# Encoder trunk on one core: the engine that evacuates a transpose is picked by slot instead of by a running count

## The chip, the cores and the metric

The kernel runs on one core of a Trainium2 chip. The metric is device time of one execution, in microseconds (us). The engines are PE (matmuls and transposes), DVE (VectorE), ACT (ScalarE), POOL (GpSimd) and SP, which only issues DMAs here.

## What is computed

Two layers of an encoder over 2048 tokens of width 1024, float32. Each layer normalises x, projects it, runs four groups of attention heads (A dense, B sliding window, C neighbourhood with a bias, D differential), gates each, and projects back:

```python
h = _rmsnorm(x, norm_g[l]); z = h @ w_in[l]
o_a = dense softmax(q_a k_a^T) v_a            # 4 query heads on 2 key-value heads
o_b = softmax over a window of +-128 keys, with a sink logit
o_c = softmax over an 8 x 16 neighbourhood, with rpb_c
o_d = (softmax(q1 k1^T) - lam * softmax(q2 k2^T)) v_d
mix = concat(o_a*silu(g_a), o_b*silu(g_b), o_c*silu(g_c), o_d*silu(g_d))
x = x + mix @ w_out[l]
```

## The kernel before

Tokens go in 16 tiles t of 128. A layer has four stages: the D projections (with the output projection of the layer before), D attention with the other projections threaded in, the phase of the A, B and C heads, and the output projection. The change is in the third, which takes about 530 us of each layer.

That phase makes two **sweeps** over the 16 query tiles. Sweep 1 pairs A's key-value head 0 with the B heads, sweep 2 pairs A's key-value head 1 with the C heads. One query tile of a sweep is a **group** of three units: an A unit (two query heads against 2048 keys) and two small units (two heads each, three blocks of 128 keys for B, three or four of 120 for C). A unit has scores (S, Sb or Sc, matmuls into PSUM), a maximum and a copy to SBUF on DVE (L497, L1007, L1043), one `exp` on ACT per head (L504 for A, 2048 wide; L1018 and L1051 for the small units), transposes of the probabilities on PE, an evacuation of the transposes from PSUM to SBUF, and the product with v (L520, L539).

`drive` writes PE's order by hand, and in this phase PE keeps that order. It runs one group's transposes while it computes the next group's scores. A **slot** is one call of `front`: up to four transposes into one PSUM tile PTp (L513 or L531), an evacuation, then one score unit of the next group. The A unit has slots 0 to 7 of a group, the first small unit slots 8 and 9, the second slots 10 and 11 (in groups 0 and 15 of sweep 1 the small units have one slot each: 8 and 9). After the last slot come the products L520 and L539, and then the next group's slot 0. `k_build` puts four transposes of keys (kT, L98) ahead of slot 3 or slot 6 in sweep 1: one build in groups 1, 3, 4, 6 and 9, two in groups 5 and 11 to 14. A build of B or C keys takes four steps on ACT and DVE in turn (L959, L960, L962, L963), one of A keys two (L962, L963).

PTp tiles come from `tpool`, which hands out two turns of a PSUM pool of two buffers (it also holds kT) and then one of a pool of one. Scores have three PSUM buffers. Only PE's order is fixed: DVE, ACT, POOL and SP take the order that a scheduler gives them when the program is built, so the change moves instructions there.

Evacuations go through `evac`. Its third argument was a period: `ev[0]` counts all evacuations of a layer, D's 256 included, and every third goes to DVE (L472), the rest to ACT (L474):

```python
ev[0] += 1
if mode and ev[0] % mode == 0:
    V.tensor_copy(dst, src)
else:
    A.copy(dst, src)
```

As a group has twelve slots, the count falls on the same slots again and again: 0, 3, 6 and 9 in groups 1 to 15 of sweep 1, and 2, 5, 8 and 11 in sweep 2 (1, 4 and 7 in group 0 of sweep 1). All D evacuations have mode 0 and are ACT's.

Of the kernel before, what the change touches and what calls it, by code (L numbers as in the profile page):

```python
# [27 lines left out]
GAP2 = 2  # L28
GAP3 = 0
KQ = 5  # L30
EVB = 3
EVC = 3
MS0 = 2
WPT = 13
WOU = 360
KA0 = 16
FR2 = 12.2
EV3 = 3
EVA1 = 3
SC64 = 64.0 ** -0.5  # L40
SC32 = 32.0 ** -0.5
NEG = -1e30
# [35 lines left out]
def trunk_kernel(ctx, tc, x, norm_g, w_in, w_out, qn_a, kn_a, sink_b, rpb_c, lam_q1, lam_k1, lam_q2, lam_k2,  # L78
# [180 lines left out]
    for l in range(depth):  # L259
# [91 lines left out]
        dv = dvx.enter_context(tc.tile_pool(name="dv", bufs=2, reuse_waits="tile"))  # L351
        with tc.tile_pool(name="wd", bufs=16, reuse_waits="tile") as wp, tc.tile_pool(name="st", bufs=3, reuse_waits="tile") as st:
# [84 lines left out]
            for t in range(NT):  # L437
                h = hs.pop(t)
                if t == WPT:
                    wb = big.tile([128, 4, 2, 256], F32R, tag="b", name="wb")  # L440
                    for k in range(4):
                        s = st.tile([128, 384], F32, tag="st", name="wst")
# [17 lines left out]
        with tc.tile_pool(name="sm", bufs=6, reuse_waits="tile") as sm, \  # L460
# [1 line left out]
                tc.tile_pool(name="sps", bufs=3, space=PSUM, reuse_waits="tile") as sps, tc.tile_pool(name="ops", bufs=1, space=PSUM, reuse_waits="tile") as ops, \  # L462
                tc.tile_pool(name="tps2", bufs=2, space=PSUM, reuse_waits="tile") as tps:
            later = []
            ev = [0]
            vt, kt = {}, {}
            tpool = cycle([tps])

            def evac(dst, src, mode):
                ev[0] += 1  # L470
                if mode and ev[0] % mode == 0:
                    V.tensor_copy(dst, src)  # L472
                else:
                    A.copy(dst, src)  # L474
# [32 lines left out]
            def dense_front(u, i):  # L507
                p, c = u["p"], slice(i * 256, (i + 1) * 256)
                tp = next(tpool).tile([128, 512], F32, tag="t", name="PTp")
                for h in range(2):  # L510
                    for a in range(2):
                        j = i * 2 + a
                        PE.transpose(tp[:, (h * 2 + a) * 128:(h * 2 + a + 1) * 128], p[:, h, j * 128:(j + 1) * 128], idn)  # L513
                evac(p[:, :, c], tp.rearrange("p (h k) -> p h k", h=2), u["ev"])

            def dense_back(u):
                js = range(NT) if u["fixed"] else range(NT - 1, -1, -1)
# [5 lines left out]
            def small_front(u, i):  # L523
                ws, n, kw = u["ws"], u["n"], u.get("kw", 128)
                js = [j for j in (2 * i, 2 * i + 1) if j < n]
                if i == 0:
                    u["pt"] = u["ptp"].tile([128, 1024], F32, tag="pt", name="PT")
                tp = next(tpool).tile([128, 512], F32, tag="t", name="PTp")
                for a, j in enumerate(js):
                    for h in range(2):  # L530
                        PE.transpose(tp[0:kw, (a * 2 + h) * 128:(a * 2 + h + 1) * 128], ws[h][:, j * kw:(j + 1) * kw], idn)  # L531
                w = len(js) * 256
                evac(u["pt"][0:kw, i * 512:i * 512 + w], tp[0:kw, 0:w], u["ev"])

            def small_back(u):
                n, kw = u["n"], u.get("kw", 128)
# [188 lines left out]
            with tc.tile_pool(name="st2", bufs=5, reuse_waits="tile") as st, tc.tile_pool(name="w2", bufs=10, reuse_waits="tile") as wp, \  # L725
# [177 lines left out]
                with tc.tile_pool(name="bb", bufs=1, reuse_waits="tile") as bbp, tc.tile_pool(name="p1", bufs=1, reuse_waits="tile") as p1p:  # L903
                    kds = {(0, 0): kd0[0], (0, 1): kd0[1]}

                    def get_kd(kv):
                        def f(c):
                            if (kv, c) not in kds:
                                k_ = big2.tile([128, S], F32R, tag="b", name="kdt")
                                nc.sync.dma_start(out=k_.bitcast(F32), in_=kd_d[0][:, c, :])  # L910
                                kds[kv, c] = k_
                            return kds[kv, c]
                        return f
                    units = [dict(kv=kv, t=t, k=get_kd(kv), qp=dv, s=d_scores, par=True, ns=16, nv=8, ev=0, fin=fin_d, fb=6 + kv,
                                  p1=p1p, fixed=False, front=dense_front, back=dense_back, get_o=own_o,
                                  v=lambda h, j, kv=kv: vd[:, j, kv * 64:(kv + 1) * 64]) for kv in range(2) for t in range(NT)]

                    for u in units:
                        u["fp"] = lambda: tps.tile([128, 512], F32, tag="t", name="fin")
                    for u in units[-2:]:  # L920
                        u["fp"] = lambda: zps.tile([128, 256], F32, tag="z", name="fin")
                    drive([[u] for u in units], GAP2, fill, FR2)
# [133 lines left out]
                yield  # L1056

            def a_unit(kv, t, q, pre):
                return dict(kv=kv, t=t, s=a_scores, par=True, ev=EVA1 if kv else EV3, ns=8, nv=8, fin=fin_plain, fb=kv, q=q, pre=pre,
                            front=dense_front, back=dense_back, get_o=own_o, oc=0, fixed=True, fd=4,  # L1060
                            v=lambda h, j: vt["A"][:, j, kv * 64:(kv + 1) * 64])

# [5 lines left out]
            o_bc = []  # L1068

            def small_unit(sc, i, t, q, px, fb, ns, nv, bias=None, pre=lambda: None):  # L1070
                return dict(kv=i, t=t, s=sc, par=False, ev=EVC if sc is c_scores else EVB, ns=ns, nv=nv, fin=fin_plain, fb=fb, q=q, pp=px, bias=bias, pre=pre,
                            front=small_front, back=small_back, get_o=pair_o, oc=128 * i, ptp=ptp, fd=5 + 2 * i)

            with tc.tile_pool(name="qst", bufs=2, reuse_waits="tile") as qst, tc.tile_pool(name="ql", bufs=2, reuse_waits="tile") as ql, \
# [63 lines left out]
                units = []  # L1138
                for ps in range(2):
                    for t in range(NT):  # L1140
                        units.append(a_unit(ps, t, lambda t=t, ps=ps: qq["A", ps, t], lambda t=t, ps=ps: prep(ps, t + 1)))
                        for i in range(2):
                            if ps == 0:
                                units.append(small_unit(b_scores, i, t, lambda t=t: qq["B", 0, t], px, 2 + i, 2,
                                                        (min(t + 2, NT) - max(t - 1, 0) + 1) // 2))
                            else:
                                units.append(small_unit(c_scores, i, t, lambda t=t: qq["C", 1, t], px, 4 + i, 2, 2,
                                                        lambda t=t, i=i: get_bias(t, i)))
                                units[-1]["cm"] = cm
# [49 lines left out]
```

## Time and profile before

| | |
|---|---|
| Time, median of 3 runs (lowest, highest) | 3598.17 us (3595.62, 3601.56) |
| The profiled execution's own time | 3600.7 us |
| Its span in the trace | 3598.7 us |
| Busy: PE, DVE, ACT, POOL | 3449.8, 2503.0, 2097.6, 955.6 us |
| Granted clock of PE, mean | 0.986 |

The span is from the first to the last instruction; the 2.0 us between it and the time lie around the trace. A busy PE is one that has a matmul in its pipeline, and the ends of matmuls are modelled, so lost time shows better in the distance between two starts than in the idle time.

### The profile page before, as it was taken

The numbers are of one execution on the slowest core, as the hardware profiler recorded it, in microseconds if no ns is written. First come the engines' busy times: TensorE is split into PE (matmuls) and PEld (weight loads), VectorE is DVE, ScalarE is ACT, GpSimd is POOL, SyncE is SP. The second block draws the span as 40 slices with busy tenths as digits, with TensorE's granted clock in tenths as the row PEclk, the third lists the DMA queues.
The fourth block names the chain that finished last, engine by engine and source line by source line (L and its number), as shares of the span: only waits on it lengthen the run. The fifth ranks groups of instructions, "written<-read, shape, count | busy, mean of one in ns | idle before, by whom it ended". The sixth has DMA issues, their size and how long they took to land. (4 is left out here: it accounts for less than half of the span.)

```text
span 3598.7 us, 71627 instructions
## 1 busy us (share of the span) xinstructions
PE 3449.8 (96%) x25232; PEld 2969.7 (83%) x25232; DVE 2503.0 (70%) x7829; ACT 2097.6 (58%) x3961; POOL 955.6 (27%) x1604
## 2 busy tenths in 40 slices
PE   8989999999989999999999899999999799899999
PEld 8979898888967777877899798988889577678787
DVE  4387878777877887774234878787777787777733
ACT  4455666556667776771144556665666677777711
POOL 4465324643100001001044553255331100000000
PEclk9999999999999999999999999999999999999999
DMA  4542325332233244335445323253231332543343
GB/s 146 186 113 85 85 80 175 86 91 77 62 95 84 81 122 121 88 100 178 147 132 180 96 79 92 70 181 88 79 87 57 97 86 82 135 111 96 90 158 113
DMA packets 355777, 387.47 MB, mean 108 GB/s; under 512 B 59802, under 2 KB 298586, under 8 KB 350298
## 3 DMA queue, kind: packets, MB, share of 16 engines
q1 hardware_dynamic: 351098, 367.17, 35.1%
q10 hardware_dynamic: 4320, 15.73, 1.3%
q8 instruction: 199, 3.26, 0.4%
q14 instruction: 160, 1.31, 0.1%
HBM read 258.83 MB, written 123.91 MB: 106 GB/s over the span
## 5 line engine op out<-in xcount | busy, mean ns | idle before, releaser
L497 DVE TENSOR_SCALAR_CACHE_REDUCE P<-S 128x512 f32<-128x512 f32 x1536 | 1018.5, 686 | 238.8 <-PE S L496 172.4
L319 PE MATMUL z<-wt,ht 128*128 128x256 f32 (+1 forms) x3008 | 892.5, 298 | 8.6 <-ACT wt L310 4.1
L321 PE MATMUL z<-wt,ht 128*128 128x256 f32 (+1 forms) x3008 | 885.5, 295 | 4.0 <-DVE wt L313 4.0
L323 PE MATMUL z<-wt,ht 128*128 128x256 f32 (+1 forms) x3008 | 884.1, 294 | 0.0
L513 PE MATMUL PTp<-idr,P 128*128 128x128 f32 x4096 | 632.3, 278 | 38.9 <-ACT P L474 19.8
L474 ACT COPY P<-PTp 128x512 f32<-128x512 f32 x864 | 491.3, 584 | 291.9 <-PE PTp L513 289.0
L504 ACT ACTIVATE P<-P,nm 128x2048 f32<-128x2048 f32 x256 | 513.8, 2007 | 180.5 <-DVE jk L503 172.1
L513 PEld LDWEIGHTS PTp<-idr,P 128*128 128x128 f32 x4096 | 495.4, 143 | 137.0 <-ACT P L474 28.0
L319 PEld LDWEIGHTS z<-wt,ht 128*128 128x128 f32 x3008 | 570.1, 190 | 28.4 <-ACT wt L310 4.5
L321 PEld LDWEIGHTS z<-wt,ht 128*128 128x128 f32 x3008 | 571.0, 190 | 18.4 <-DVE wt L313 6.2
L323 PEld LDWEIGHTS z<-wt,ht 128*128 128x128 f32 x3008 | 570.9, 190 | 7.0
L496 PE MATMUL S<-kA,q 128*128 128x512 f32 x1024 | 364.1, 438 | 8.3 <-DVE P L497 8.3
L222 PE MATMUL y<-wot,ms 128*128 128x512 f32 x1440 | 331.1, 392 | 0.6 <-DVE ms L212 0.6
L222 PEld LDWEIGHTS y<-wot,ms 128*128 128x128 f32 x1440 | 270.7, 188 | 60.7 <-DVE ms L212 1.0
L544 POOL TENSOR_TENSOR gg<-gt,rzh 128x128 f32<-128x128 f32 x192 | 77.3, 403 | 911.7 <-DVE rzh L606 385.9
L312 POOL TENSOR_SCALAR wt<-wst,g 128x256 fp32r<-128x256 f32 (+1 forms) x336 | 215.2, 652 | 363.8 <-PE z L323 263.0
L721 DVE SCALAR_TENSOR_TENSOR P<-P,cf,P 128x2048 f32<-128x2048 f32 x128 | 306.0, 2391 | 2.7
L504 ACT ACTIVATE P<-P,nm,rr_a 128x2048 f32<-128x2048 f32 x128 | 268.6, 2098 | 33.5 <-DVE jk L503 32.4
L520 PE MATMUL O<-P,vd 128*64 128x256 f32 x2048 | 238.8, 385 | 0.8 <-ACT P L474 0.7
L520 PE MATMUL O<-P,vA 128*64 128x256 f32 x2048 | 236.8, 384 | 0.0
L313 DVE SCALAR_TENSOR_TENSOR wt<-wst,g,wt 128x256 fp32r<-128x256 f32 (+1 forms) x344 | 195.9, 599 | 37.3 <-POOL wt L312 34.3
L496 PE MATMUL S<-kdt,qd 128*128 128x512 f32 x512 | 213.4, 439 | 8.3 <-DVE P L497 5.8
(195 smaller groups left out, 5150.2 us busy)
## 6 DMA issues: line engine op xcount, KB each, us to landing
wst<-in_w_in_dram SPq DMA_DIRECT2D x320, 128.0 KB
qd<-qd SPq DMA_DIRECT2D x128, 128.0 KB
htd<-ht SPq DMA_DIRECT2D x16, 1024.0 KB
ht<-htd SPq DMA_DIRECT2D x16, 1024.0 KB
q<-qsA SPq DMA_DIRECT2D x128, 128.0 KB
q<-qsB SPq DMA_DIRECT2D x64, 256.0 KB
q<-qc SPq DMA_DIRECT2D x64, 256.0 KB
mload<-mx ACTq DMA_DIRECT2D x30, 512.0 KB
```

The lines of the kernel that those rows point to most:

```text
L222: PE.matmul(ys[c], lhsT=ms[:, a, kc], rhs=wts[k][:, b, c * 512:(c + 1) * 512], start=(k == 0 and i == 0), stop=(k == KD - 1 and i == 2))
L312: G.tensor_scalar(wt[:, 0, :], s, g8[:, k:k + 1], 0.0, op0=ALU.mult, op1=ALU.add)
L319: PE.matmul(z, lhsT=h[:, 0, kc], rhs=wk[:, 0, :], start=(k == 0), stop=False)
L321: PE.matmul(z, lhsT=h[:, 0, kc], rhs=wk[:, 1, :], start=False, stop=False)
L323: PE.matmul(z, lhsT=h[:, 1, kc], rhs=wk[:, 0, :], start=False, stop=(k == KD - 1))
L474: A.copy(dst, src)
L496: PE.matmul(s, lhsT=q, rhs=k_ap[:, c:c + 512], start=(i == 0), stop=(i == len(q_list) - 1))
L497: V.tensor_scalar(p[:, c:c + 512], s, 1.0, None, op0=ALU.mult, op1=ALU.max, accum_out=mx[:, j:j + 1])
L504: A.activation(p, p, ACTF.Exp, bias=nm, scale=scale, accum_out=zacc)
L513: PE.transpose(tp[:, (h * 2 + a) * 128:(h * 2 + a + 1) * 128], p[:, h, j * 128:(j + 1) * 128], idn)
L520: PE.matmul(u["o"][a * 64:(a + 1) * 64, 0:256], lhsT=u["v"](0, j), rhs=u["p"][:, :, j * 128:(j + 1) * 128], start=(n < 2), stop=(n >= NT - 2))
L721: V.scalar_tensor_tensor(p0, p1, cf, p0, op0=ALU.mult, op1=ALU.add)
```

## The change

`evac` is told by its caller which engine to use. Each unit has a set of its own slots that go to DVE: the A unit its slots 5 and 6, the first small unit none, the second both of its own, which are slots 10 and 11 of a group. D's set is empty, as its period was 0. Line numbers of the changed file are up to 6 lower: L472, L474, L497, L503, L504 and L963 are L466, L468, L491, L497, L498 and L957 there.

```diff
-EVB = 3
-EVC = 3
...
-EV3 = 3
-EVA1 = 3
...
-            ev = [0]
...
-            def evac(dst, src, mode):
-                ev[0] += 1
-                if mode and ev[0] % mode == 0:
+            def evac(dst, src, on_v):
+                if on_v:
                     V.tensor_copy(dst, src)
                 else:
                     A.copy(dst, src)
...
-                evac(p[:, :, c], tp.rearrange("p (h k) -> p h k", h=2), u["ev"])
+                evac(p[:, :, c], tp.rearrange("p (h k) -> p h k", h=2), i in u["ev"])
...
-                evac(u["pt"][0:kw, i * 512:i * 512 + w], tp[0:kw, 0:w], u["ev"])
+                evac(u["pt"][0:kw, i * 512:i * 512 + w], tp[0:kw, 0:w], i in u["ev"])
...
-    qp=dv, s=d_scores, par=True, ns=16, nv=8, ev=0, fin=fin_d, fb=6 + kv,
+    qp=dv, s=d_scores, par=True, ns=16, nv=8, ev=(), fin=fin_d, fb=6 + kv,
...
-    return dict(kv=kv, t=t, s=a_scores, par=True, ev=EVA1 if kv else EV3, ns=8, ...
+    return dict(kv=kv, t=t, s=a_scores, par=True, ev=(5, 6), ns=8, ...
...
-    return dict(kv=i, t=t, s=sc, par=False, ev=EVC if sc is c_scores else EVB, ns=ns, ...
+    return dict(kv=i, t=t, s=sc, par=False, ev=(0, 1) if i else (), ns=ns, ...
```

In the built program the phase has 254 evacuations on DVE before (160 of A, 94 of small units) and 252 after (128 and 124).

ACT, group 8 of sweep 1 (no build), before: P is A's probabilities, PT the small units'; L504 are the two wide exponentials of the next group.

```order
L474 COPY P<-PTp 128x2x256 x4
L504 ACTIVATE P,zt<-P,nm,rr_a 128x2048
L474 COPY P<-PTp 128x2x256
L474 COPY PT<-PTp 128x512 x2
L504 ACTIVATE P,zt<-P,nm,rr_a 128x2048
L474 COPY PT<-PTp 128x256
```

The same stretch after the change.

```order
L468 COPY P<-PTp 128x2x256 x5
L498 ACTIVATE P,zt<-P,nm,rr_a 128x2048
L468 COPY P<-PTp 128x2x256
L468 COPY PT<-PTp 128x512
L468 COPY PT<-PTp 128x256
L498 ACTIVATE P,zt<-P,nm,rr_a 128x2048
```

ACT now copies slots 0 to 4 ahead of the first exponential, slots 7 to 9 between the two, and nothing behind the second.

DVE, group 11 of sweep 1 (two builds of C keys), before: from the first copy of the group to the end of the first build's last step; kC are the key tiles, mix a finished output times its gate, L503 the bias that the exponential waits for.

```order
L472 COPY P<-PTp 128x2x256
L497 TENSOR_SCALAR P,mx<-S 128x512 x3
L472 COPY P<-PTp 128x2x256
L960 TENSOR_TENSOR kC_16542<-kT,kC_16542 64x512
L497 TENSOR_SCALAR P,mx<-S 128x512
L552 TENSOR_TENSOR mix<-O,os 128x128
L497 TENSOR_SCALAR P,mx<-S 128x512
L552 TENSOR_TENSOR mix<-Obc,os 128x128
L963 TENSOR_TENSOR kC_16543<-kT,kC_16543 64x512
L503 TENSOR_SCALAR jk,nm<-mx,nrr_a 128x4
L497 TENSOR_SCALAR P,mx<-S 128x512
L960 TENSOR_TENSOR kC_16544<-kT,kC_16544 64x512
```

The same stretch after the change, up to the second build's first step.

```order
L491 TENSOR_SCALAR P,mx<-S 128x512 x3
L954 TENSOR_TENSOR kC_16542<-kT,kC_16542 64x512
L491 TENSOR_SCALAR P,mx<-S 128x512
L546 TENSOR_TENSOR mix<-O,os 128x128
L497 TENSOR_SCALAR jk,nm<-mx,nrr_a 128x4
L957 TENSOR_TENSOR kC_16543<-kT,kC_16543 64x512
L491 TENSOR_SCALAR P,mx<-S 128x512
L466 COPY P<-PTp 128x2x256
L546 TENSOR_TENSOR mix<-Obc,os 128x128
L491 TENSOR_SCALAR P,mx<-S 128x512
L466 COPY P<-PTp 128x2x256
L954 TENSOR_TENSOR kC_16544<-kT,kC_16544 64x512
```

DVE has no copy ahead of the fifth score, the bias L503 (L497 in the changed file) and the first build's last step stand one score earlier, and the copies of slots 5 and 6 stand between the scores 4, 5 and 6.

## Rows read from the trace of the kernel before

**Rows 1.** Busy time by stretch, sweep 1 of layer 0: length, then busy us per engine, clock, DMA.

```profile
core 0: us, PE busy (x) PEld busy (x) DVE busy (x) ACT busy (x) POOL busy (x), PEclk, DMA share, GB/s
1096.00:1344.40 248.40, 236.73 (x1926) 188.09 (x1924) 200.06 (x747) 192.39 (x412) 17.28 (x43) 1.00 0.36 95
```

**Rows 2.** Waits of PE in layer 0, sweep 1, then sweep 2: total us, times, longest.

```profile
PE PTp L531 <- ACT PT L474: 4.8, 5, 1.7
...
PE S L496 <- DVE P L497: 8.3, 1, 8.3
PE Obc L549 <- DVE jk L503: 0.7, 4, 0.2
```

**Rows 3.** Timeline of PE: start of the products of groups 4 to 11, sweep 1.

```profile
1165.55 3.67 PE L520 MATMUL O<-P,vA 128*64 128x256 f32 x32
...
1183.75 3.67 PE L520 MATMUL O<-P,vA 128*64 128x256 f32 x32
...
1200.17 3.67 PE L520 MATMUL O<-P,vA 128*64 128x256 f32 x32
...
1215.49 3.67 PE L520 MATMUL O<-P,vA 128*64 128x256 f32 x32
...
1230.81 3.67 PE L520 MATMUL O<-P,vA 128*64 128x256 f32 x32
...
1247.94 3.67 PE L520 MATMUL O<-P,vA 128*64 128x256 f32 x32
...
1263.26 3.67 PE L520 MATMUL O<-P,vA 128*64 128x256 f32 x32
...
1282.20 3.67 PE L520 MATMUL O<-P,vA 128*64 128x256 f32 x32
```

**Rows 4.** The instructions on tile PTp: count, then shortest, median and longest ns.

```profile
L474 ACT COPY P<-PTp x864: 559/587/642, 219.4 to 3403.8; 128x512 f32<-128x512 f32 x173
...
L472 DVE COPY P<-PTp x160: 674/689/693, 1087.9 to 3401.8; 128x512 f32<-128x512 f32 x160
```

**Rows 5.** Timeline of group 6, sweep 1 (one build): start, us, engine, idle before.

```profile
1188.67 0.66 PE L513 MATMUL PTp<-idr,P 128*128 128x128 f32 x4
...
1189.36 0.69 DVE L472 COPY P<-PTp 128x512 f32<-128x512 f32 x1 [0.63 <-PE PTp L513]
...
1195.70 0.60 PE L513 MATMUL PTp<-idr,P 128*128 128x128 f32 x4
...
1195.95 2.10 ACT L504 ACTIVATE P<-P,nm,rr_a 128x2048 f32<-128x2048 f32 x1 [0.94 <-DVE jk L503]
...
1196.44 0.69 DVE L472 COPY P<-PTp 128x512 f32<-128x512 f32 x1
...
1197.04 0.68 DVE L497 TENSOR_SCALAR_CACHE_REDUCE P<-S 128x512 f32<-128x512 f32 x1
...
1198.66 0.66 PE L531 MATMUL PTp<-idr,Pb 128*128 128x128 f32 x4 [0.26 <-ACT P L474]
```

**Rows 6.** Timeline of group 11, sweep 1 (two builds): PE, then DVE, then ACT.

```profile
1274.77 0.54 PE L98 MATMUL kT<-idr,kl 128*128 128x128 f32 x4 [0.30 <-ACT P L474]
1275.93 0.66 PE L513 MATMUL PTp<-idr,P 128*128 128x128 f32 x4 [0.63 <-DVE kC L963]
...
1280.12 0.44 PE L531 MATMUL PTp<-idr,Pb 128*128 128x128 f32 x2 [0.75 <-ACT PT L474]
...
1275.19 0.69 DVE L963 TENSOR_TENSOR kC<-kT,kC 64x512 fp32r<-64x512 f32 x1
...
1276.17 2.10 ACT L504 ACTIVATE P<-P,nm,rr_a 128x2048 f32<-128x2048 f32 x1 [0.25 <-DVE jk L503]
```

**Rows 7.** Timeline of PE in a group of sweep 2, layer 0.

```profile
1507.60 0.30 PE L549 MATMUL Obc<-idr,gg 128*128 128x128 f32 x1 [0.17 <-DVE jk L503]
```

**Rows 8.** Timeline of DVE where sweep 1 of layer 0 ends.

```profile
1357.33 0.17 DVE L279 TENSOR_SCALAR nsnk<-snk 128x4 f32<-128x4 f32 x1 [8.89 <-DMA snk<-in_sink_b_dram]
```

**Rows 9.** Busy time by stretch, right behind that wait; columns as in rows 1.

```profile
1358.00:1364.00 6.00, 5.84 (x23) 5.32 (x24) 4.39 (x19) 1.20 (x3) 0.00 (x0) 0.50 0.31 87
```

**Rows 10.** Timeline of PE in the phase's last group, layer 0.

```profile
1618.76 1.14 PE L513 MATMUL PTp<-idr,P 128*128 128x128 f32 x8 [0.96 <-ACT P L474]
```

More of the change, by code (lines that the diff above doesn't have):

```diff
@@ L913, in get_kd @@
                         return f
-                    units = [dict(kv=kv, t=t, k=get_kd(kv), qp=dv, s=d_scores, par=True, ns=16, nv=8, ev=0, fin=fin_d, fb=6 + kv,
+                    units = [dict(kv=kv, t=t, k=get_kd(kv), qp=dv, s=d_scores, par=True, ns=16, nv=8, ev=(), fin=fin_d, fb=6 + kv,
                                   p1=p1p, fixed=False, front=dense_front, back=dense_back, get_o=own_o,
@@ L1058, in a_unit @@
             def a_unit(kv, t, q, pre):
-                return dict(kv=kv, t=t, s=a_scores, par=True, ev=EVA1 if kv else EV3, ns=8, nv=8, fin=fin_plain, fb=kv, q=q, pre=pre,
+                return dict(kv=kv, t=t, s=a_scores, par=True, ev=(5, 6), ns=8, nv=8, fin=fin_plain, fb=kv, q=q, pre=pre,
                             front=dense_front, back=dense_back, get_o=own_o, oc=0, fixed=True, fd=4,
@@ L1070, in small_unit @@
             def small_unit(sc, i, t, q, px, fb, ns, nv, bias=None, pre=lambda: None):
-                return dict(kv=i, t=t, s=sc, par=False, ev=EVC if sc is c_scores else EVB, ns=ns, nv=nv, fin=fin_plain, fb=fb, q=q, pp=px, bias=bias, pre=pre,
+                return dict(kv=i, t=t, s=sc, par=False, ev=(0, 1) if i else (), ns=ns, nv=nv, fin=fin_plain, fb=fb, q=q, pp=px, bias=bias, pre=pre,
                             front=small_front, back=small_back, get_o=pair_o, oc=128 * i, ptp=ptp, fd=5 + 2 * i)
```

## The prediction, made before the changed kernel was run

> **What bounds the kernel now.** I read the busy time by stretch first. In sweep 1 of layer 0 PE is busy 236.73 of 248.40 us, DVE 200.06 and ACT 192.39 [rows 1]: PE bounds the phase, and the change can only win what PE loses there. The list of waits says what it loses to: in sweep 1 mostly transposes that wait for an evacuation, in sweep 2 almost nothing but one wait of 8.3 us [rows 2]. The list understates it, since PE's pipeline drains and refills around each wait, so I take the distance between the starts of two groups' products. Groups 7, 8 and 10, with no build of keys, take 15.32 us each; group 6 takes 16.42, group 5 18.20, group 9 17.13 and group 11 18.94 [rows 3]. A build adds four transposes, busy for 0.54 us when alone [rows 6] and overlapping the next ones by about 0.1, so I put it at 0.43. Then the groups with one build of A keys lose 16.42 - 15.32 - 0.43 = 0.67 us, that with one build of B keys 1.38, group 5 with two 2.02, and group 11 2.76. Per layer: three of the first kind (3, 4, 6), two of the second (1, 9), one of the third, four of the fourth (11 to 14): 2.0 + 2.8 + 2.0 + 11.0 = **17.8 us**, and twice that for two layers. Groups without a build lose nothing, and that is the stock from which the change can draw.
>
> **Where a loss comes from.** Group 6 shows it. Slot 0 starts at 1188.67 and slot 7 at 1195.70. The first wide exponential holds ACT from 1195.95 for 2.10 us. Slot 6 is DVE's, which reaches it only at 1196.44; slot 7 is ACT's and waits for the exponential's end. The small unit's transposes at 1198.66 wait for slot 7's copy [rows 5]. The exponential itself is late (7.28 us after slot 0) because its bias stands behind the fifth score on DVE.
>
> **The change, part by part.**
>
> *Work per engine.* DVE has 252 copies instead of 254, of the same shapes to within 32 that pass between A and the small units; at 689 ns on DVE against 587 on ACT [rows 4] the totals move by under 2 us over the phase on engines that are 20% idle [rows 1]. Cost: nothing, covered by that idle time; without it 2 us.
>
> *Groups with one build of A keys (3, 4, 6).* I replay group 6 in the new order. An evacuation can start 0.69 us after its transposes (1189.36 against 1188.67), DVE takes one copy or score per 0.60 us (1196.44 to 1197.04) [rows 5]. DVE now has three scores, the build's L963, the fourth score and then the bias, which is done about 5.6 us after slot 0. ACT has copied slots 0 to 4 by 5.4, so the exponential runs from 5.6 to 7.7 instead of 7.3 to 9.4. Slots 5 and 6 are done on DVE at 6.9 and 8.3, slot 7 on ACT at 8.3; PE needs their buffers from 8.0, 8.8 and 9.4 on. Nothing waits: gain 0.66 each, 2.0 per layer.
>
> *Groups with one build of B keys (1, 9).* The build's last step ends at 6.3, the copies of slots 5 and 6 at 7.6 and 9.0. Slot 6's transposes wait 0.25 for the kT buffer, the second small score 0.42 for a score buffer. Of 1.35 lost, 0.7 stays: gain 0.6 each, 1.2 per layer.
>
> *Group 5.* Slot 6 waits 0.4 for slot 5's copy, slot 9 0.5 for slot 8's: gain 1.1.
>
> *Groups 11 to 14.* Before, the second kT waits for slot 5's copy on ACT at 1274.77, slot 6 at 1275.93 for the first build's last step (1275.19), slot 9 for slot 8's copy at 1280.12 [rows 6]. The new order ends that last step about 1.4 us earlier and starts the exponential at 5.8 us after slot 0 instead of 8.0. But slot 5's copy now stands on DVE behind that step and the fifth score, and ends at 7.6: the second kT starts about 1.0 us later than before. Later slots win that back: slot 9's wait falls from 1.2 to 0.7, and the products start some 0.5 earlier. Gain 0.5 each, 2.0 per layer. This is the term I trust least: the ends are 0 and 2.76 per group.
>
> *Sweep 1 together.* 2.0 + 1.2 + 1.1 + 2.0 = 6.3 per layer, **12.5 us** in all, with 0 and 35.6 as ends.
>
> *Groups without builds, and sweep 2.* By the same replay all buffers come free in time; the tightest is the second small score's, 0.3 us before PE wants it, and 0.1 where output weights are split in the same group. In sweep 2 a transposed output waits in four groups per layer for DVE to read the first one (0.17 idle, 0.35 by the distance) [rows 2, 7]. The new order reads it ahead of the sixth score: 4 x 0.35 x 2 = **2.8 us** gained.
>
> *Last group.* No scores lie between its transposes, and PE already waits 0.96 for ACT [rows 10]. ACT now takes slots 0 to 4 in a row where slot 2 was DVE's, one more copy of about 0.5 us in the chain: **1.0 us** lost over two layers, between 0 and 2.
>
> *The end of sweep 1 in layer 0.* DVE waits 8.89 us for a tiny load of the next layer's constants that lies behind large loads in the DMA queues [rows 8]; PE stands still with it and then has a granted clock of 0.50, the 1.2 GHz level, for 6 us [rows 9]. The load is still issued behind the same loads, but DVE now takes one more score and one multiply first, so PE gets one slot further: **0.9 us** gained. If the load came in time it would be 8.3 + 3; if it came later by a transfer, 2 lost.
>
> *Queues.* On SP a gate load moves behind a store of outputs, and half of a query load ahead of one; neither is used before the next group, so I put both at nothing; the cover is a whole group, some 15 us. In layer 1's D stage the scheduler swaps some twenty matmuls around one score; I put it at 0, within 1 either way.
>
> **Sum.** 12.5 + 2.8 + 0.9 - 1.0 = 15.2 us less. The profiled execution's own 3600.7 becomes 3585.5. It lies 2.5 above the median of the three runs, so against 3598.17 I expect **3583 us**.
>
> **Rivals.**
>
> *The buffers, not the engine, make the bubbles.* In groups 11 to 14 a kT holds one of two buffers for five microseconds, whoever copies. Then those groups gain nothing: 15.2 - 4.0 = 11.2, and 3587 us. For it speaks the replay, in which the second kT starts later; against it the wait at 1280.12, which an earlier exponential does shorten [rows 6]. The Trainium skill, "Perfetto Trace Analysis", section "Optimization Strategy", says that the same gap repeating on the engine that should be saturated can mean there is not enough SBUF or PSUM for the next tile. By that rule these groups keep their 2.76 us whole, and the time is this rival's.
>
> *All of it goes.* If both copies keep ahead of PE, sweep 1 gives 35.6: 3598 - 35.6 - 2.8 - 0.9 + 1.0 = 3560. For it speaks that the exponential starts two microseconds earlier everywhere; against it that builds hold ACT and DVE in turn.
>
> *Nothing comes of it.* The count is the same and only places move: waits for ACT become waits for DVE in sweep 1, as in the second kT, and only sweep 2's 2.8 us is left, less the last group's: 3596.
>
> *DVE falls behind.* Slots 5 and 6 go to DVE back to back and 10 and 11 too, among the small scores. If DVE is later than the replay by more than 0.3 us there, the second small score waits for its buffer in every group that has no wait today: fifteen of sweep 2 and four of sweep 1 per layer, 38 in all. At the 0.66 that one wait costs in group 6 this is 25 us lost against 15.2 gained: 3608. Against it, DVE has a fifth of its time free [rows 1].
>
> **How the numbers follow.** My forecast has 0.47, the buffers 0.17, all of it 0.10, nothing 0.18, DVE behind 0.08. A measurement of this kernel can tell about 0.2%, 7 us, from no change. The forecast, the buffers and the full gain are faster by more, but for 0.05 of chance in the first two; nothing is within 0.2%; DVE behind is slower. That gives 0.69 faster, 0.23 the same, 0.08 slower. The range takes in the forecast, the buffers, nothing with its ends of 2 us, and below the forecast 15 of the 18 us that groups 11 to 14 leave open (8 x 2.26): 3568 to 3598; the full gain and a late DVE are left out.
>
> **What would show it.** In the changed profile, groups 3, 4 and 6 take 15.75 us and groups 11 to 14 about 18.4; the exponential of group 6 starts under 6 us after slot 0; in group 11 the second kT waits for DVE instead of ACT. Groups of sweep 2 keep their length and lose the wait of the transposed output. Groups longer than before in sweep 2, or PE waiting for L491 ahead of L999 or L1036 (the small scores) there, would make it wrong; so would groups 11 to 14 as long as the others.

## The result, and the profile after

| | before | after |
|---|---|---|
| Median (lowest to highest), 5 runs each | 3598.17 us (3595.62 to 3601.56) | 3580.12 us (3577.66 to 3582.80) |
| The profiled execution's own time | 3600.7 | 3577.66 |
| Its span | 3598.7 | 3575.9 |

The ratio is 0.9949 with a 95% interval of 0.9938 to 0.9960: 18.05 us less where 15.2 had been forecast. The two profiled executions lie further apart, 23.0 us, so the account of the trace has to say where the other five come from.

First the busy time, of the whole execution (the page's part 1) and of a stretch of sweep 1 of layer 0, from the first products to 3.9 us behind those of group 14; the last row is the same stretch before, with the same 1871 matmuls ([rows 1] begin earlier and end later).

```profile
PE 3440.1 (96%) x25232; PEld 2967.9 (83%) x25232; DVE 2501.2 (70%) x7827; ACT 2111.0 (59%) x3963; POOL 954.5 (27%) x1604
```

```profile
1095.90:1331.90 236.00, 228.71 (x1871) 183.56 (x1872) 194.81 (x726) 190.20 (x402) 17.22 (x43) 1.00 0.36 96
```

```profile
1100.71:1342.57 241.86, 230.19 (x1871) 182.43 (x1872) 194.27 (x724) 186.85 (x402) 17.28 (x43) 1.00 0.36 95
```

PE still is the engine that is full: 228.71 of 236.00 us, 97% for 95%. DVE has 83% for 80%, ACT 81% for 77%; the work is the same in 5.9 us less. PE's waits in that stretch, and under them those of the rest of the phase, answer to [rows 2]:

```profile
PE PTp L507 <- DVE P L466: 3.6, 5, 0.8
PE PTp L525 <- ACT PT L468: 2.6, 5, 0.7
PE Obc L543 <- DVE mix L546: 0.4, 2, 0.2
...
PE Sc L1036 <- DVE P L491: 8.0, 1, 8.0
```

Seven kinds of waits, of which [rows 2] show the longest, have become three. The starts of the products of groups 4 to 11, PE's timeline, answer to [rows 3]:

```profile
1159.25 3.67 PE L514 MATMUL O<-P,vA 128*64 128x256 f32 x32
...
1176.51 3.67 PE L514 MATMUL O<-P,vA 128*64 128x256 f32 x32
...
1192.39 3.67 PE L514 MATMUL O<-P,vA 128*64 128x256 f32 x32
...
1207.71 3.67 PE L514 MATMUL O<-P,vA 128*64 128x256 f32 x32
...
1223.03 3.67 PE L514 MATMUL O<-P,vA 128*64 128x256 f32 x32
...
1239.74 3.67 PE L514 MATMUL O<-P,vA 128*64 128x256 f32 x32
...
1255.07 3.67 PE L514 MATMUL O<-P,vA 128*64 128x256 f32 x32
...
1273.37 3.67 PE L514 MATMUL O<-P,vA 128*64 128x256 f32 x32
```

Group 5 takes 17.26 us, group 6 15.88, groups 7, 8 and 10 15.32 or 15.33, group 9 16.71, group 11 18.30. All lengths below are such distances; in both kernels layer 1 repeats layer 0's within 0.03 us in groups 1 to 14, so a difference of 0.1 in one group means something although it is far below what the whole time can tell.

Timeline of groups 6 and 11 of sweep 1 (PE, ACT and DVE picked out; [rows 5, 6]):

```profile
1181.43 0.66 PE L507 MATMUL PTp<-idr,P 128*128 128x128 f32 x4
...
1187.21 2.10 ACT L498 ACTIVATE P<-P,nm,rr_a 128x2048 f32<-128x2048 f32 x1 [0.46 <-DVE jk L497]
...
1187.71 0.68 DVE L466 COPY P<-PTp 128x512 f32<-128x512 f32 x1
...
1189.11 0.68 DVE L466 COPY P<-PTp 128x512 f32<-128x512 f32 x1
...
1189.31 0.56 ACT L468 COPY P<-PTp 128x512 f32<-128x512 f32 x1
...
1259.98 0.66 PE L507 MATMUL PTp<-idr,P 128*128 128x128 f32 x4
...
1265.64 0.69 DVE L957 TENSOR_TENSOR kC<-kT,kC 64x512 fp32r<-64x512 f32 x1
...
1266.39 0.54 PE L94 MATMUL kT<-idr,kl 128*128 128x128 f32 x4
1267.72 0.66 PE L507 MATMUL PTp<-idr,P 128*128 128x128 f32 x4 [0.80 <-DVE P L466]
...
1271.18 0.44 PE L525 MATMUL PTp<-idr,Pb 128*128 128x128 f32 x2 [0.55 <-ACT PT L468]
```

In group 6 the exponential starts 5.78 us after slot 0 instead of 7.28, the copies of slots 5, 6 and 7 all end by 1189.9, and the profile lists no wait of PE. In group 11 the second kT starts at 6.41 after slot 0 (6.59 before), just behind the first build's last step; slot 6 waits 0.80 for slot 5's copy and starts at 7.74, where it stood before (7.75); the second transposes of the small unit start at 11.20 instead of 11.94. What the group gains, it gains late.

The sweep's end and the last group, [rows 8, 10]:

```profile
1347.28 0.17 DVE L275 TENSOR_SCALAR nsnk<-snk 128x4 f32<-128x4 f32 x1 [9.14 <-DMA snk<-in_sink_b_dram]
...
1605.28 0.66 PE L507 MATMUL PTp<-idr,P 128*128 128x128 f32 x4 [0.68 <-ACT P L468]
1607.36 0.66 PE L507 MATMUL PTp<-idr,P 128*128 128x128 f32 x4 [1.43 <-ACT P L468]
...
1606.20 0.62 ACT L251 CAST wot<-wos 128x512 fp32r<-128x512 f32 x1 [0.98 <-DMA wos<-in_w_out_dram]
1606.73 1.55 ACT L468 COPY P<-PTp 128x512 f32<-128x512 f32 x3
```

**The account of the two spans, 22.8 us.** 2.9 of it lies ahead of the first slot of group 0 in layer 0, where every engine runs the same instructions in the same order in both kernels. There PE's clock differs between the executions; this is the busy time by stretch at 860 us, before and then after (columns as in [rows 1]):

```profile
865.00:870.00 5.00, 5.00 (x27) 4.93 (x26) 1.48 (x11) 2.21 (x3) 0.71 (x1) 0.56 0.42 107
```

```profile
865.00:870.00 5.00, 5.00 (x42) 4.82 (x42) 4.33 (x19) 3.41 (x6) 1.11 (x2) 1.00 0.32 70
```

Before, the granted clock is 0.56 there, near the 1.2 GHz level, and 27 matmuls start in five microseconds; after, 1.00 and 42. It is chance: in the ten traces whose engines run exactly the same instructions up to there, this slot starts anywhere between 1082.36 and 1088.74.

Another 1.9 is group 0 of sweep 1 itself, 15.41 us from its first slot to its products before and 13.54 after. PE waits there for a product of the gate on POOL (gg), which needs a small step on DVE (s); before, DVE's copy of slot 1 stands ahead of that step. Timelines of PE and DVE, before and then after:

```profile
1091.25 0.45 PE L549 MATMUL fin<-idr,gg 128*128 128x128 f32 x1 [3.12 <-POOL gg L544]
...
1087.91 0.69 DVE L472 COPY P<-PTp 128x512 f32<-128x512 f32 x1
...
1088.58 0.15 DVE L593 TENSOR_TENSOR s<-fin,rz 128x2 f32<-128x2 f32 x1
```

```profile
1087.75 0.33 PE L543 MATMUL fin<-idr,gg 128*128 128x128 f32 x1 [2.57 <-POOL gg L538]
...
1085.04 0.15 DVE L587 TENSOR_TENSOR s<-fin,rz 128x2 f32<-128x2 f32 x1
```

This wait is 3.11 to 3.14 us in both layers of every trace in which DVE copies slot 0 or slot 1 of that group, and 2.57 in all others: 0.55 per layer is won by the slots. The other 1.3 here is the clock again, 0.57 behind the wait before and 1.00 after.

Then come 7.28 in layer 0's phase and 8.93 in layer 1's, 16.2 together, and 1.8 between and behind them (0.3 of it in group 0 of layer 1). The 16.2 are: 11.7 in groups 1 to 14 of sweep 1, 0.86 at the end of sweep 1 of layer 0, 2.4 in groups 2 to 14 of sweep 2, less 1.95 in the last groups, and 3.2 that had no term, in the first two groups of sweep 2 (0.47 in layer 0, 2.73 in layer 1).

### The profile page after: what moved, and what is told of

Its sections match the earlier page's. It is cut to its first block, busy times and chain, and to the rows that moved or that the text cites. A ratio compares the mean times of both kernels' runs of the same rounds, so it can differ in the third digit from the quotient of the medians.

```text
span 3575.9 us, 71599 instructions
## 1 busy us (share of the span) xinstructions
PE 3440.1 (96%) x25232; PEld 2967.9 (83%) x25232; DVE 2501.2 (70%) x7827; ACT 2111.0 (59%) x3963; POOL 954.5 (27%) x1604
## 5 line engine op out<-in xcount | busy, mean ns | idle before, releaser
L491 DVE TENSOR_SCALAR_CACHE_REDUCE P<-S 128x512 f32<-128x512 f32 x1536 | 1025.6, 685 | 263.6 <-PE S L490 195.2
L468 ACT COPY P<-PTp 128x512 f32<-128x512 f32 x896 | 511.4, 585 | 220.0 <-PE PTp L507 215.7
L498 ACT ACTIVATE P<-P,nm 128x2048 f32<-128x2048 f32 x256 | 513.9, 2008 | 182.7 <-DVE jk L497 173.9
L498 ACT ACTIVATE P<-P,nm,rr_a 128x2048 f32<-128x2048 f32 x128 | 268.5, 2098 | 63.1 <-DVE jk L497 60.7
L490 PE MATMUL S<-kd,qd 128*128 128x512 f32 x512 | 208.8, 429 | 12.5 <-DVE P L491 10.9
```

The lines of the kernel that those rows point to most:

```text
L490: PE.matmul(s, lhsT=q, rhs=k_ap[:, c:c + 512], start=(i == 0), stop=(i == len(q_list) - 1))
L491: V.tensor_scalar(p[:, c:c + 512], s, 1.0, None, op0=ALU.mult, op1=ALU.max, accum_out=mx[:, j:j + 1])
L498: A.activation(p, p, ACTF.Exp, bias=nm, scale=scale, accum_out=zacc)
```

## The experiments

Every trace gives the lengths of the groups in sweep 1 and 2; this table holds those that decide (us, layer 0, unless both layers are given). The kernel before was run again beside each batch of versions, with medians of 3598.00 to 3601.04; the ratios are to those runs.

| version | 7, 8, 10 | 3, 4, 6 | 9 | 5 | 11 to 13 | 14 | 15 | sweep 2, groups 8, 10, 12 | last, both layers | layer 1, first two of sweep 2 | time, median | ratio to before, 95% |
|---|---|---|---|---|---|---|---|---|---|---|---|---|
| before | 15.32 | 16.41 | 17.13 | 18.20 | 18.94 | 18.59 | 26.26 | 16.95 | 12.96, 13.00 | 38.40 | 3598.17 | |
| after | 15.32 | 15.88 | 16.71 | 17.26 | 18.30 | 18.04 | 25.40 | 16.58 | 14.07, 13.84 | 35.67 | 3580.12 | 0.9938 to 0.9960 |
| e1: sweep 1 alone | 15.32 | 15.88 | 16.71 | 17.26 | 18.30 | 18.05 | 25.36 | 16.95 | 13.31, 13.22 | 37.75 | 3583.05 | 0.9941 to 0.9966 |
| e2: sweep 2 alone | 15.32 | 16.41 | 17.13 | 18.20 | 18.93 | 18.59 | 25.55 | 16.58 | 14.47, 14.23 | 36.91 | 3596.91 | 0.9984 to 1.0002 |
| e3: A at 0, 3 | 15.68 | 16.41 | 17.14 | 19.56 | 20.12 | 20.02 | 24.67 | 16.58 | 14.09, 15.10 | 35.24 | 3615.52 | 1.0025 to 1.0056 |
| e4: small 8, 9 | 15.64 | 16.38 | 17.21 | 18.31 | 19.12 | 18.77 | 25.35 | 16.58 | 13.99, 14.58 | 36.76 | 3599.98 | 0.9992 to 1.0010 |
| e5: last as before | 15.32 | 15.88 | 16.72 | 17.25 | 18.30 | 18.06 | 25.57 | 16.58 | 13.05, 11.83 | 35.16 | 3583.30 | 0.9939 to 0.9968 |
| e6: sink constants | 15.33 | 15.87 | 16.71 | 17.26 | 18.30 | 18.05 | 14.78 | 16.56 | 13.76, 14.86 | 36.04 | 3580.19 | 0.9935 to 0.9965 |
| e9: slot 5 on ACT | 15.32 | 15.88 | 16.72 | 18.75 | 18.64 | 19.90 | 25.14 | 16.58 | 14.35, 14.17 | 36.98 | 3596.69 | 0.9982 to 1.0006 |
| f1: before, cleared | 15.33 | 16.41 | 17.14 | 18.20 | 18.93 | 18.60 | 14.78 | 16.95 | 13.14, 13.15 | 30.51 | 3583.94 | 0.9949 to 0.9973 |
| f2: after, cleared | 15.33 | 15.87 | 16.71 | 17.27 | 18.30 | 18.06 | 14.78 | 16.57 | 14.26, 14.66 | 30.51 | 3570.41 | 0.9909 to 0.9937 |
| f3: f2, last as before | 15.33 | 15.87 | 16.71 | 17.25 | 18.31 | 18.05 | 14.78 | 16.57 | 12.86, 11.84 | 30.51 | 3565.32 | 0.9895 to 0.9921 |

**e1 and e2, one sweep at a time.** The old slots are put back in one sweep.

```diff
 e1: - ev=(5, 6)             + ev=(2, 5) if kv else (5, 6)
     - ev=(0, 1) if i else () + C units: (1,) if i else (0,)
 e2: - ev=(5, 6)             + ev=(5, 6) if kv else (0, 3, 6) if t else (1, 4, 7)
     - ev=(0, 1) if i else () + B units: () if i else (1,)
```

(In e2 the one-slot units of groups 0 and 15 follow the old count too.) Expected of e1:

> The change in sweep 1 alone; sweep 2 keeps the old slots (2, 5 of A, 8 and 11). Theory (the exponential's bias comes earlier on DVE, so the gain sits in sweep 1's groups with builds): groups 1, 3 to 6, 9 and 11 to 14 as short as in the changed kernel (16.28, 15.88, 17.26, 16.71, 18.30), 11.7 us over both layers, the last group back at 13.0 (2 us won against the changed kernel), the four groups of sweep 2 back at 16.95 (2.5 lost): about 3583 us. Rival (most of the gain was the granted clock ahead of the phase and luck with transfers): under 6 us, 3592 or more.

and of e2:

> The change in sweep 2 alone; sweep 1 keeps the old slots. Theory: sweep 1's groups as before (16.41, 18.94), three groups of sweep 2 per layer at 16.56 for 16.95, the last groups 14.0: the two cancel, so 3598 within 2 us. The 2.7 us that layer 1's first two groups of sweep 2 gained (stores of mix) tell whose they are: with sweep 2's slots they stay (3595), with sweep 1's they go. Rival (sweep 2 carries the gain): 3585 or less.

Measured: 3583.05 and 3596.91. In groups 1 to 14 each sweep's lengths follow its own slots to 0.02 us, whatever the other has. So sweep 1 carries the change, sweep 2's gain and the last groups' loss all but cancel, and what is gained in groups 1 to 14 is neither the clock nor transfers. The turn of the sweeps in layer 1 was not decided: 38.40 before, 37.75 with sweep 1's slots, 36.91 with sweep 2's, 35.67 with both.

**e3, A's copies at slots 0 and 3.**

```diff
-  ev=(5, 6)
+  ev=(5, 6) if kv else (0, 3)
```

> The changed kernel with A's DVE slots of sweep 1 at 0 and 3 for 5 and 6, so as many copies on DVE, and the small units' at 10 and 11 as they are. Theory (copies of slots 0 and 3 stand ahead of the bias on DVE and make the exponential late): groups 3, 4 and 6 back at 16.3 to 16.5, groups 11 to 14 at 18.8 or more, the exponential of group 6 at 7 us or later after slot 0 for 5.78; 8 to 12 us of sweep 1's 11.7 lost, about 3590. Rival (the small units' slots or the even split bring the gain, wherever A's slots are): groups 3, 4, 6 at 15.9, 3580.

Measured 3615.52, slower than the kernel before. The exponentials are late again (7.28 after slot 0 in group 6), but the loss is far larger than expected, and it hits groups without a build, which the old slots left alone. Group 7's timeline shows it:

```profile
1219.17 0.44 PE L525 MATMUL PTp<-idr,Pb 128*128 128x128 f32 x2
...
1216.46 2.10 ACT L498 ACTIVATE P<-P,nm,rr_a 128x2048 f32<-128x2048 f32 x1
...
1218.56 1.05 ACT L468 COPY P<-PTp 128x512 f32<-128x512 f32 x2
```

Slots 6 and 7 are both ACT's now and both stand behind the exponential; slot 9's transposes start at 1219.17, when the first of the two copies is done. Before, slot 6 was DVE's. So the two A copies on DVE have to be those that fall into the exponential's two microseconds, besides being away from the bias. How much of the loss is the late exponential and how much slot 6 is not told apart here.

**e4, the other small unit.**

```diff
-  ev=(0, 1) if i else ()
+  B units: () if i else (0, 1)
```

> The changed kernel with sweep 1's small copies on DVE those of the first small unit (slots 8 and 9) for the second's (10 and 11). Theory (A's slots 5 and 6 carry the gain): groups 3, 4 and 6 stay at 15.9 within 0.2, groups 11 to 14 at 18.3 within 0.4: 3580 within 3 us. Rival (the second small unit's slots matter, since ACT then copies them behind the second exponential, 2.1 us late): every group waits for slot 10's copy, 0.5 us or more in each of 30 groups, 3595 or more.

Measured 3599.98: no gain is left, and my theory that A's slots carry it fell. Group 6 has its early exponential (5.79 after slot 0) and yet takes 16.38. Its timeline:

```profile
1191.53 0.66 PE L507 MATMUL PTp<-idr,P 128*128 128x128 f32 x4
...
1201.98 0.44 PE L525 MATMUL PTp<-idr,Pb 128*128 128x128 f32 x2
...
1197.32 2.10 ACT L498 ACTIVATE P<-P,nm,rr_a 128x2048 f32<-128x2048 f32 x1 [0.47 <-DVE jk L497]
...
1201.24 0.69 DVE L466 COPY PT<-PTp 128x512 f32<-128x512 f32 x1
```

DVE, still busy with slots 5 and 6 and A's last scores, reaches slot 8's copy at 1201.24 and ends it at 1201.93; slot 11's transposes start right behind it. With slots 10 and 11 DVE may be as late as that: in group 6 of the changed kernel it ends them at 1192.9 and 1193.7, and what PE does meanwhile, from 1192.39 on, is five microseconds of products. So the rival's time came, but by DVE's copy of slot 8 and not by ACT's of slot 10. With as many copies on DVE, neither half of the new assignment wins by itself. (No run changes how many copies DVE takes.)

**e5, the last group as before.**

```diff
-  ev=(5, 6)
+  ev=(2, 5) if kv and t == NT - 1 else (5, 6)
-  ev=(0, 1) if i else ()
+  C units of t == NT - 1: (1,) if i else (0,)
```

> The changed kernel with the old slots (2, 5, 8, 11) in the last group of each layer alone. Theory (in the last group no scores lie between the transposes and one more copy in a row on ACT costs PE about 1 us): the last groups 13.0 for 14.07 and 13.84, 1.9 us less, 3578. Rival (the last group ends with the output weights or the products of the next stage, which wait for something else): 3580.

The last groups fall to 13.05 and 11.83, as expected and more in layer 1; the time, 3583.30 (3576.11 to 3586.03), can't show 3 us. f3 repeats it on a quieter ground.

**e6 and e8, the turn of the sweeps.** e6 gives `snk` and `nsnk` two buffers, e8 gives mix four, in the kernel before.

```diff
 e6: - tag="snk", name="snk")   + tag="snk", name="snk", bufs=2)     (nsnk the same)
 e8: - tag="m", name="mix")     + tag="m", name="mix", bufs=4)
```

> The changed kernel with two buffers for the sink constants and their negative, so the next layer's 128x4 load is issued at the program's start. Theory (in layer 0 PE's wait of 8.0 us at the end of sweep 1 is DVE's for this load, behind large loads in the queues, and the 0.9 us that the change gained there is the work that DVE does ahead of it): that wait goes, group 15 of sweep 1 falls from 25.4 to 15 or 16, 9 to 10 us less, about 3570. Rival (the loads that the small one lies behind are themselves needed, and the wait moves to them): 3 us or less, 3577 or more.

> The kernel before with four buffers for a finished output (mix) in place of two, every engine's order as it was. In layer 1 DVE waits 4.88 and 1.93 us at the start of sweep 2 for stores of mix, and the first two groups of sweep 2 take 21.04 and 17.36 us; in the changed kernel, which issues loads and stores in another order on SP, there is no such wait and they take 20.01 and 15.66. Theory (these 2.7 us are the stores' and not the evacuations'): the wait goes here too, the two groups take 20.0 and 15.7, and all else stays: 3595.5. Rival (the groups gain by the new slots): they stay at 21.0 and 17.4, 3598.

In e6 the wait for the small load is gone and group 15 takes 14.78, but the time stays at 3580.19. Waits of DVE, from 1330 us on, in e6:

```profile
DVE mix L546 <- DMA mx<-mix: 5.2, 1, 5.2
```

The next thing that the queues hold up is a store: DVE may not overwrite a mix tile until it has left, and group 0 of sweep 2 now takes 20.01 instead of 14.83. So of 10.6 us 5.4 go in the trace. The time does not show them; in the profiled execution the first products stand at 1105.21, 9.3 later than the changed kernel's, which hides more than that. Layer 1 had that wait all along, before (first) and after:

```profile
DVE mix L552 <- DMA mx<-mix: 6.8, 2, 4.9
```

```profile
DVE mix L546 <- DMA mx<-mix: 5.2, 1, 5.2
```

e8 takes it away: 38.40 falls to 30.49, and the time to 3592.88 (0.9978 to 0.9996). That is 7.9 us, not the 2.7 expected: the change had only shortened this wait, and "no such wait" in the expectation was misread. (In e8 the last group of layer 0 takes 16.54: ACT waits 2.13 us there for a load of output weights, L255, ahead of its copies.)

**e7, one build of C keys to a group.** Loads start at t = 8, one pair of heads each, in place of two from t = 12 on.

```diff
-  if ps == 0 and t >= 12:
-      loaded.append(("C", t - 12, k_load(ql, "C", t - 12)))
+  if ps == 0 and t >= 8:
+      loaded.append(("C", (t - 8) // 2, k_load(ql, "C", (t - 8) // 2, t % 2)))
```

> The changed kernel with the eight builds of C keys spread one to a group over groups 7 to 14 of sweep 1, in place of two in each of 11 to 14 (group 9 then has two with its B build). Theory (what groups 11 to 14 still lose is slot 5's copy behind a build on DVE, and a second build in a group costs more than a first): groups 11 to 14 at 16.3 to 16.7 for 18.30, groups 7, 8 and 10 at the same for 15.32, group 9 at 18.3: 2 us less per layer, 3576. Rival (a build costs 1.5 us wherever it stands, as a tile of keys holds one of two buffers): no change, 3580.

Groups 7, 10 and 11 to 13 take 16.70 or 16.71, group 9 18.30, group 14 16.48; group 8, which also waited 1.3 us behind a store, 18.24. Groups 7 to 14 of layer 0 sum to 136.6 us against 135.6: nothing won, 3583.67 (0.9944 to 0.9973). The rival is right: the first C build of a group costs 1.38, the second 1.60, wherever they stand. Group 10 shows what it consists of:

```profile
1258.40 0.46 PE L94 MATMUL kT<-idr,kl 128*128 128x128 f32 x4
...
1262.04 0.66 PE L507 MATMUL PTp<-idr,P 128*128 128x128 f32 x4
1263.79 0.30 PE L543 MATMUL Obc<-idr,gg 128*128 128x128 f32 x1 [0.18 <-DVE mix L546]
...
1261.29 0.69 DVE L957 TENSOR_TENSOR kC<-kT,kC 64x512 fp32r<-64x512 f32 x1
```

The keys hold a PSUM buffer from 1258.40 until the fourth step of the build ends at 1261.98, and slot 6 starts when it does. By the distances from slot to slot, against group 7 of the changed kernel, that is 0.27 of the 1.38 us; 0.44 are the build's own transposes, and the rest is DVE, which is late with a transposed output (0.34) and with a score behind it (0.22). So the time is the rival's, but the buffer that the keys hold is the smaller part of it. A build of A keys has two steps, holds its buffer from 1184.19 to 1185.99 in group 6, and costs 0.56.

**e9, slot 5 on ACT where two builds are.**

```diff
-  ev=(5, 6)
+  ev=(6,) if kv == 0 and t in (5, 11, 12, 13, 14) else (5, 6)
```

> The changed kernel with slot 5 on ACT in the groups with two builds (5 and 11 to 14 of sweep 1). Theory (in them slot 6 waits 0.80 us for slot 5's copy on DVE, and that copy is what sets the length there): ACT takes the copy behind the first exponential, ends it 0.6 later than DVE does, and these groups grow by 0.5 to 0.7 us, 6 us in all, 3586. Rival (a tile of keys holds one of the two buffers whoever copies): they stay at 17.26 and 18.30 within 0.1, 3580.

Groups 11 to 13 grow by 0.34, between the two theories: slot 6 waits 1.45 instead of 0.80, and a later wait falls from 0.55 to 0.3. The time is 3596.69 over ten runs, 16.6 more than after, of which these groups explain 2 over both layers. Group 5 grew by more, 1.5 in layer 0 and 2.9 in layer 1 (slot 6 waits 1.92 and 1.91 there), and so did 14 in layer 0; in the trace the ten groups grow by 8.6 together. PE's timeline in e9, the same wait in group 12 and in group 14, and the clock right behind each:

```profile
1292.09 0.66 PE L507 MATMUL PTp<-idr,P 128*128 128x128 f32 x4 [1.45 <-ACT P L468]
...
1329.37 0.94 PE L507 MATMUL PTp<-idr,P 128*128 128x128 f32 x4 [1.46 <-ACT P L468]
```

```profile
1292.00:1294.00 2.00, 1.92 (x13) 1.56 (x13) 1.43 (x3) 1.22 (x4) 0.00 (x0) 1.00 0.62 163
...
1330.00:1332.00 2.00, 2.00 (x10) 1.70 (x8) 1.86 (x4) 0.58 (x1) 0.00 (x0) 0.50 0.00 0
```

Behind the second one the granted clock is 0.50, the 1.2 GHz level, and the group takes 19.90 instead of 18.39 (group 14 of layer 1). Group 5 of layer 1 is the only other of the ten groups where this happens:

```profile
2959.00:2961.00 2.00, 2.00 (x9) 1.67 (x8) 1.93 (x6) 0.67 (x2) 0.00 (x0) 0.50 0.00 0
```

That this happens more often in the slower executions is likely but not shown, as only one of them was profiled.

**f1, f2 and f3, without the transfers.** f1 is the kernel before and f2 the changed one, both with the edits of e6 and e8; f3 is f2 with that of e5.

> The kernel before with two buffers for the sink constants and four for mix, so that neither load nor store is waited for at the turn of the sweeps; the engines' order is the same but for one tiny operation. Theory: group 15 of sweep 1 in layer 0 falls from 26.26 to 14.8 and the first two groups of sweep 2 in layer 1 from 38.4 to 30.5, 19 us less, 3579. Rival (the queues are full there, and something else that they carry is waited for next): 8 us or less, 3590 or more.

> The changed kernel with the same two edits, so that against the former it shows what the slots alone are worth. Theory (the engines' part is 11.7 in sweep 1 and 2.5 in sweep 2 gained, 1.9 in the last groups lost): 12.3 us less than the kernel before with the edits, and group 15 of layer 0 and group 0 of sweep 2 in layer 1 at 14.8, 15.8 us less than the changed kernel: 3564 to 3567. Rival (part of the change's 18 us came through the transfers, and goes with their waits): under 8 us between the two; or (all of it is the engines') 18.

> The former with the old slots in the last group of each layer. Theory: the last groups 1 to 2 us shorter each than in the former, 2 to 3 us less in all, 3562, the fastest of the versions. Rival (the last groups' length is set by transfers that run there): the same time as the former.

Measured 3583.94, 3570.41 and 3565.32. Both edits together take 14 us from the kernel before (19 expected, and 19.8 by the two phases of its trace, which begin 2.8 later), where e6's alone showed nothing on the changed one. f2 lies 9.7 below the changed kernel, where 15.8 was expected: its two phases are 15.2 shorter, but begin 7.7 later. Between f1 and f2 lie 13.5 us, and 12.7 by their traces (5.96 and 5.60 in the two phases, 1.1 in group 0 of the two layers): the slots' own worth, against 12.3 expected. f3 takes another 5.1 us, where 2 to 3 was expected (4.2 by the last groups of the two traces), and beats both kernels of this case: 0.9908 of before, 33 us.

## Why the prediction was right

The sum held, 15.2 against 18.05 with an interval of 14 to 22, and the mechanism with it. But its terms measure 13.0 together; the other 5 us came from places for which it had no gain, so that the total lies this close is partly luck. These steps did not hold as written.

- **Sweep 1, 12.5: measured 11.7.** Groups 3, 4 and 6 gained 0.54 each (0.66 forecast), 1 and 9 0.42 (0.6), 5 0.94 (1.1), 11 to 14 0.62 (0.5). The replay of group 6 was right to 0.2 us in its main number, an exponential at 5.78 for "about 5.6". "Nothing waits" was nearly right: the group is still 0.13 longer than forecast, of which the build, 0.45 for 0.43, is little; 0.1 arises behind slot 9, where a small score is a little late. In groups 1 and 9 slot 6 did follow the build's last step, but a transposed output waits next, 0.19 for DVE, and the second small score is 0.2 late instead of 0.42. The sum gives slots 10 and 11 no share; e4 shows that without them nothing of the gain is left.
- **Groups 11 to 14, the least trusted term.** The gain came out right by a wrong step: "the second kT starts about 1.0 us later than before" is false, it starts 0.18 earlier, since it follows the build's last step and not slot 5's copy. Slot 6 is the one that waits for that copy, and so starts where it did. That later slots win back was right (11.20 for 11.94).
- **Sweep 2, 2.8: measured 2.4.** Three groups per layer gained 0.38, the fourth 0.08. I took four as equal.
- **Group 0, nothing: 1.1.** "Groups without a build lose nothing" left this group out. Its wait for the gate's product was shortened by 0.55 in each layer, as DVE has no copy ahead of the step that it needs.
- **Last group, 1.0 lost: measured 1.95,** and 1.4 and 2.8 in the two layers between f2 and f3. I counted one more copy once. PE now waits twice, 0.68 and 1.43 for one wait of 0.96 [rows 10], and the second is not for copies alone: ACT makes the copy that PE wants at 1606.73, behind a cast of output weights for whose load it waited 0.98. In f3 the last group of layer 0 (12.86) has such a wait of 0.85 on ACT ahead of its copies, that of layer 1 (11.84) has none. So part of the loss comes through a load, and its size is chance: over the fourteen traces the old slots take 11.83 to 13.31 and once 16.54 (e8), the new 13.76 to 15.10.
- **End of sweep 1, 0.9: measured 0.86.** That they agree is luck. With the old slots in sweep 1 this group takes 26.26, 25.55 (e2) and 24.30 (e8), with slots 5 and 6 from 25.05 to 25.57, so when the load comes moves it by more than the term. And I treated the load as the whole of that wait. e6 shows a store right behind it, and half of what the load's removal gave went there.
- **Queues, nothing: 3.2.** The cover that I named, "a whole group", does not exist at the turn of the sweeps, where DVE waits for stores, in layer 1 for 6.8 us before and 5.2 after. The versions with two mix buffers lie between 35.2 and 38.4 there, all with four at 30.5. How much of the difference is the change's order on SP and how much chance stays open.

Of the rivals, *the buffers* fell as it was put: these groups gained 0.62. What group 11 has left, 2.98 us over a group without builds, is by the distances 0.8 for the builds' own transposes, 0.3 behind the first build's last step, where the keys hold a buffer, 1.0 for slot 5's copy on DVE, 0.7 for slot 8's on ACT, and 0.2 that is spread. Whether more buffers would take these waits away is not shown, as no run adds one. The rule of the Trainium skill ("Perfetto Trace Analysis", section "Optimization Strategy"), that such a gap can mean too little SBUF or PSUM, is therefore not tested here for what is left; the part that the change won, 0.62, came with the same buffers. *DVE behind* did not come, and e4 shows how near it was: the same number of DVE copies two slots earlier cost 0.32 us in each group without a build, by a copy that DVE reaches late.

## What to carry to other kernels

Give the copy that can be late to the engine that is behind, and put it where the waiting engine has long work of its own next: here slots 10 and 11 ahead of five microseconds of products. Look at what one engine does for long at a stretch (the exponential) and hand over exactly the copies that fall into it; an equal share by count lands on the operation that others wait for, and moving the same number of copies to the wrong slots cost about 33 us (e3 lies 14.5 above the kernel before, the change 18.05 below). Look also at what else an engine has in its row: a copy behind a cast that waits for a load comes as late as the load. A wait for one transfer should be costed together with the next thing in the same queue.

## What was not expected of the hardware

The same wait of 1.45 us left the clock at 1.00 in one group and was followed by 0.50 in another, for a further 1.5 us; of the ten waits of 1.45 to 1.92 us in e9's trace two were followed by it. And with the same instructions ahead of it, group 0's first slot began anywhere within 6.4 us, with stretches of the granted clock near 0.5 that come in one execution and not in the next: this is more than most edits of this case are worth, so that lengths of groups in one trace tell more than medians of five times.
